# Gate sums moved from DMA to DVE, the last norm cut into 512-column pieces, and one product instead of two per sample in a hybrid decoder step

## The chip, the cores and the metric

The kernel runs on one core of one Trainium2 chip. The metric is device time in microseconds of one execution, the median of several runs. A core has five engines that run side by side and wait for one another only through semaphores: TensorE (PE in the profile; its weight loads are listed apart as PEld), VectorE (DVE), ScalarE (ACT), GpSimd (POOL) and SyncE (SP). Each takes its instructions in the order in which they were written. Transfers are issued from the queues of SP, POOL and ACT and are carried by 16 DMA engines. PE writes its results into PSUM; the others work mostly on SBUF.

## The reference

One layer of a decoder with three recurrent mixers, for a prompt of 512 tokens and for 8 samples of one token, all in fp32:

```python
p = x @ w_in                      # 2048 -> 19464 columns, split among the mixers and 3 gates
A: S_t = diag(f_t) S_{t-1} + (1 - f_t) i_t^T,   o_t = S_t^T q_t        # 8 heads, 128 x 128
B: S_t = gamma_h S_{t-1} + k_t v_t^T,           o_t = S_t^T q_t        # 4 heads, 256 x 256
C: mLSTM matrix memory with gates and a running-max stabiliser         # 4 heads, 256 x 256
y_n = head_norm(o_n) * gain * silu(z_n)
merged = sum_n sigmoid(g_n) * (y_n @ w_branch[n])
out = merged @ w_out
x_new = LayerNorm(alpha * x + out) * ln_g + ln_b
```

Outputs are the new rows of prompt and samples, and the new states of all heads, for the prompt and for each of the 8 samples.

## The kernel before

**Dense work.** The 512 prompt columns and the 8 sample columns are handled together (N = 520, halves of 260). Each fp32 operand is split into a high part `hi` and a rest `lo` in a faster format, and a product is made of three: hi*hi, hi*lo, lo*hi. ACT writes `hi`, DVE writes `lo`. The list `items` holds the dense work; an item has one weight block of 128x1024 and 24 products (a classical item 48).

The columns of `w_in` are worked in 76 units of 256 columns, in the order A, B, C, gates; the last 24 are the gates'. The first three units are plain ("classical"), all others use a Strassen scheme with seven items instead of eight: `strassen_unit` loads the two weight blocks `r1` (b11, b12) and `r2` (b21, b22), 1 MB each, into a ring of three buffers `R`, and four sums of blocks are formed. Three are formed on DVE in place. The first, `TT = b11 + b12`, is formed by DVE in the first Strassen unit and in those with interleaved columns (`deint`: q and k of B and C); in all others by two transfers: SP loads block 0 into `TT` again from DRAM, and POOL issues a transfer of block 1 that accumulates onto it. The last item of a unit takes `TT`; it is the item called `before` when the next unit is written out, and the hooks on it (0 at its start, 2 at its middle) belong to the next unit.

Then come the three branch products and the output product, as classical items of 5.74 us, and the last unit `final_unit`, which finishes the first half of the rows before the second.

**Side work.** The heads' scans and the samples' recurrences are Python generators in three queues: `prepq`, `scanq` (prompt heads), `sampq` (samples). They put small operations between the dense products. A `yield` ends a step. `side_step` is called after every third product or so of dense work and lets each queue take one step, if the planner allows it.

**The planner.** `Clock` is a model of the engines' time that runs while the program is written. Each instruction adds its price to its engine (DVE 0.11 + 0.00107 us an element, ACT 0.15 + 0.00089, a fast product 0.00046 a column, an fp32 product 0.00085) and waits for its operands as the model has them. A queue takes its next step when the model's PE has come to the queue's due time, which is the end of the last step's work plus 0.2, and only while DVE and ACT are at most 2.0 and 2.5 us beyond `clk.next`, the expected end of the present item (2.87 us after its start). The model only sets the order of the instructions; on the chip the semaphores set the time. `need` drains queues without regard to due times. `keys` cuts the large slot tensor `SL` into pieces of 520 for the model's dependences.

**Samples of B and C** (`bc_samp`, one generator per head). For a pair of samples: ACT scales v by the two halves of k into `tm` and `vb`, DVE updates the two halves (256 columns each) of the state in its slot, POOL issues the store of the state, and PE multiplies each half with `qm[e][:, b, :]`, an 8-column mask that holds q's half in column b, adding up all samples in one PSUM tile (`os`). State and v loads for the next pair are issued ahead on SP and POOL if slots are free. The 12 slots that side work shares are taken by `sl()` and given back by `fr()`. A samples (`a_samp`) have one half only. Weight loads, state loads and reloads of parked columns share SP's queue.

**The last norm** (`norm_rows`). Rows come in two halves of two 128-row blocks. After mean and variance (DVE) and the power on POOL, each block is worked in three pieces (the last in four): ACT scales, DVE multiplies by ln_g, POOL or DVE adds ln_b, SP stores. The first half runs as a side queue entry while PE works on the second half of the final unit; the second half runs in `finish`, interleaved with the samples' norm.

All operations go through one helper, so that nearly every row of the profile has line 165 (142 and 143 for transfers); rows are told apart by the tiles' names: `PD` dense PSUM, `s` and `os` PSUM of side work, `XZ` and `X` the split activations, `R`, `TT`, `hi`, `lo` the weights, `SL` the slots, `qmt` the masks, `pk_*` parked columns, `lng`, `lnb` the norm's gain and bias.

Of the kernel before, what the change touches and what calls it, by code (L numbers as in the profile page):

```python
# [39 lines left out]
class Clock:  # L40
# [4 lines left out]
    def __init__(self):  # L45
        self.t = dict(pe=0.0, dve=0.0, act=0.0, pool=0.0, sp=0.0)
        self.pipe = 0.0
        self.w, self.r = {}, {}
        self.alias = {}
        self.latest = 0.0  # L50
        self.side = False
        self.next = 0.0
# [5 lines left out]
    def keys(self, ap):  # L58
        nm = ap.name
        nm = self.alias.get(nm, nm)  # L60
        if nm.startswith(("in_", "out_", "c_")):
            return []
        cut = CHUNK.get(nm.split("_")[0])
        if cut is None:
            return [nm]
        ext = sum(abs(st) * (n - 1) for st, n in list(ap.ap)[1:])
        return [(nm, i) for i in range(ap.offset % SPAN[nm.split("_")[0]] // cut,
                                       (ap.offset % SPAN[nm.split("_")[0]] + ext) // cut + 1)]
# [50 lines left out]
class Counted:  # L119
# [3 lines left out]
    def __getattr__(self, op):  # L123
# [22 lines left out]
        def g(*a, **kw):  # L146
# [5 lines left out]
            if me == "pe":  # L152
                if op == "transpose":
                    t = 0.109 if out.shape[-1] > 64 else 0.06
                else:
                    n = a[2].shape[-1]
                    t = max(0.06, 0.00046 * n) if a[2].dtype == F32R else max(0.06, 0.00085 * n)
            elif me == "dve":
# [15 lines left out]
def tile_hybrid_step(  # L174
# [152 lines left out]
    e8 = const.tile([128, 8, 8], F32, name="e8")  # L327
    qmt = const.tile([128, 2, 8, 8], F32, name="qmt")
    ones = const.tile([128, 1], F32, name="ones")
# [92 lines left out]
    def ralloc():  # L422
        r = RT[rcount[0] % 3]
        rcount[0] += 1
        return r

    class Item:

        def __init__(self, src, mm, post=None, keep=None, nosplit=False):
            self.src, self.mm, self.post, self.hooks = src, mm, post, {}  # L430
            self.n = len(items)
            self.keep, self.nosplit = keep, nosplit
            self.late = False
            self.part = None
            items.append(self)
# [63 lines left out]

    def strassen_unit(col, deint, fin):  # L500

        src = w_in[0][:, col:col + 256]
        u = {"o": [None, None]}
# [79 lines left out]
        added = []  # L583
        if prev and not deint:
            def blk(t):
# [68 lines left out]
    def classical_rows(src, rws, xf, fin, pre=None):  # L654

        kt = 8 * rws
        for g in range(rws):
# [69 lines left out]
    def dense():  # L727
# [5 lines left out]
        for i, it in enumerate(items):  # L733
            it.run("first")
            clk.next = clk.pe + 2.87
            if i + 1 < len(items) and not items[i + 1].late:
# [70 lines left out]

    def qmask(q, e):

        t = qmt[:, e]  # L810
        V.tensor_tensor(out=t, in0=e8, in1=q.unsqueeze(2).to_broadcast([128, NS, 8]), op=MUL)
        return t

# [207 lines left out]
    def a_samp(h):  # L1021
        q, K, f, z = sm("Aq", h), sm("AK", h), sm("Af", h), sm("Az", h)
        hb = {}
        qm = qmask(q, 0)

# [218 lines left out]
    def bc_samp(h, br):  # L1244
# [34 lines left out]
        if br == 2:  # L1279
# [4 lines left out]
            for e in range(2):  # L1284
                V.tensor_tensor(out=kn[:, :, e], in0=nt[:, :, e], in1=q[e], op=MUL)
        qm = [qmask(q[e], e) for e in range(2)]
        po = po1()
        for b0 in range(0, NS, 2):
# [6 lines left out]
            for bs in ([b0, b0 + 1],) if b0 + 1 in lds else ([b0], [b0 + 1]):  # L1295
# [16 lines left out]
                for b in bs:  # L1312
# [6 lines left out]
                    G.dma_start(out=state_out[0, b, h].rearrange("(p t) v -> p t v", t=2), in_=v3(st[:, 0:512], 2))  # L1319
                fr(tm)  # L1320
                yield 1
                for b in bs:
                    st = lds.pop(b)
                    for e in range(2):
                        T.matmul(po[0:NS, 0:256], qm[e][:, b, :], st[:, e * 256:(e + 1) * 256],
                                 start=(b == 0 and e == 0), stop=(b == 7 and e == 1))
                    fr(st)
                yield 1
            fr(vb)
# [247 lines left out]

    def w_unit(col, deint, fin):
        strassen_unit(col, deint, fin)

    def plain(nm, k0):
# [35 lines left out]
    for i, (col, deint, fin) in enumerate(wl):  # L1617
        if i < NCL:
            n1 = rcount[0]
            ralloc(), ralloc()  # L1620
            classical_w(col, fin, (n1, n1 + 1))
        else:
            strassen_unit(col, deint, fin)
    first_strassen = 4 * NCL
# [101 lines left out]
    def out_setup():  # L1726
        need("Cg", *HEADS[2])
        assert len(free["h"]) == NH and len(free["d"]) == ND, (len(free["h"]), len(free["d"]))
        out["H"] = SL[:, 0:NC * D].rearrange("p (c n) -> p c n", c=NC)
        out["ot"] = [TT.rearrange("p m n -> p (m n)")[:, 0:N], smp.rearrange("p a b -> p (a b)")[:, 0:N]]  # L1730
# [36 lines left out]
    def norm_rows(c0):  # L1767
# [8 lines left out]
        yield 1  # L1776
        for c in range(2):
            hh = H[:, c0 + c, :]
            for q0, q1, e in (((0, 672, G), (672, 1344, G), (1344, 2048, V)) if c0 + c < 3 else
                              ((0, 640, G), (640, 1152, G), (1152, 1600, V), (1600, 2048, V))):  # L1780
                qq = slice(q0, q1)
                act(out=hh[:, qq], in_=hh[:, qq], func=AF.Identity, scale=r[:, c:c + 1], bias=nm[:, c:c + 1])
                V.tensor_tensor(out=hh[:, qq], in0=hh[:, qq], in1=g[:, qq], op=MUL)
                e.tensor_tensor(out=hh[:, qq], in0=hh[:, qq], in1=b[:, qq], op=ADD)
                SY.dma_start(out=y_p[0, (c0 + c) * 128:(c0 + c + 1) * 128, qq], in_=hh[:, qq])
                yield 2

# [319 lines left out]
```

## Time and profile before

| | |
|---|---|
| runs (us) | 2373.87, 2376.09, 2375.83; median 2375.83 |
| profiled execution | 2384.39 us, span 2382.5 us, mean granted TensorE clock 0.992 |
| PE busy | 2318.9 us, 97% of the span |
| DVE, ACT, POOL busy | 1603.2, 1031.3, 490.8 us |
| transfers | 449.26 MB, 189 GB/s over the span |
| last dense product ends | at about 2352.6 us |

In the profile's rows of operations, `out<-in` names the written and the read tiles, then come partitions x elements and the count; "idle before" is the time the engine stood just before such rows, with what ended the wait. The chain of waits follows the work that ended last back from the end. Times in timelines are microseconds from the start of the span.

### The profile page before, as it was taken

The page shows a single profiled execution, that of the slowest core. Times are in us where ns is not written, and L with a number is a line of the kernel's source. Part 1 is how long each engine was busy: PE and PEld are TensorE (multiplying, and loading weights), DVE is VectorE, ACT ScalarE, POOL GpSimd, SP SyncE. Part 2 cuts the span into 40 slices and gives each one's busy share as a digit, 9 for nine tenths or more (in the row PEclk, how much of TensorE's full clock was granted, in tenths as well). Part 3 has the DMA queues.
Part 4 walks back from the last instruction along what each step waited for, and adds up shares of the span by engine and source line. Part 5 has one row for each costly group of instructions (what it writes and reads, how often), then busy time and mean ns, then how long its engine had stood idle before and what let it go on. Part 6 is the DMA issues. An engine that isn't in the chain of part 4 may idle for free.

```text
span 2382.5 us, 45461 instructions
## 1 busy us (share of the span) xinstructions
PE 2318.9 (97%) x18677; PEld 2240.8 (94%) x18677; DVE 1603.2 (67%) x2571; ACT 1031.3 (43%) x1611; POOL 490.8 (21%) x653
## 2 busy tenths in 40 slices
PE   7999999999999999999999999999999999999995
PEld 7999999999999999999999899898999999999994
DVE  5777777787778868677777666767676534553336
ACT  4344445445545444454445545554554422222222
POOL 2022221323222132222122222212221100002002
PEclk9999999999999999999999999999999999999997
DMA  6367765647566576767767988889796767755221
GB/s 178 116 158 186 196 161 170 184 151 219 149 204 167 182 213 189 223 216 205 234 184 207 187 246 203 221 200 241 169 252 173 225 201 256 253 192 199 89 72 72
DMA packets 404690, 449.26 MB, mean 189 GB/s; under 512 B 16993, under 2 KB 356865, under 8 KB 402945
## 3 DMA queue, kind: packets, MB, share of 16 engines
q1 hardware_dynamic: 313664, 312.77, 42.3%
q0 software_dynamic: 90384, 133.38, 24.2%
q8 instruction: 147, 2.41, 0.4%
q14 instruction: 63, 0.51, 0.1%
q10 hardware_dynamic: 432, 0.20, 0.0%
HBM read 362.98 MB, written 83.28 MB: 187 GB/s over the span
## 4 chain that ended last, share of the span: by engine, by line
PE 61%; DMA 3%; DVE 1%; ACT 1%; issue 0%; POOL 0%; SPq 0%; DVEq 0%; POOLq 0%; ACTq 0%
PE PD L165 54%; PE s L165 4%; PE os L165 3%; DMA R<-in_w_in_dram 1%; DVE SL L165 1%; DMA out_dram<-SL 0%; DMA R<-in_w_branch_dram 0%; DMA TT<-in_w_in_dram 0%; ACT hi L165 0%; DVE lo L165 0%; ACT SL L165 0%; ACT TT L165 0%; DVE sdd L165 0%; DVE R L165 0%; DVE fmv L165 0%
## 5 line engine op out<-in xcount | busy, mean ns | idle before, releaser
L165 PE MATMUL PD<-XZ,hi 128*128 128x260 f32 x9920 | 1430.0, 285 | 13.3 <-ACT hi L165 10.0
L165 PEld LDWEIGHTS PD<-XZ,hi 128*128 128x128 f32 x9920 | 1282.7, 189 | 30.8 <-ACT hi L165 12.0
L165 DVE TENSOR_TENSOR lo<-R,hi 128x1024 fp32r<-128x1024 f32 (+1 forms) x540 | 646.1, 1198 | 381.2 <-ACT hi L165 161.6
L165 PE MATMUL PD<-XZ,lo 128*128 128x260 f32 x4944 | 799.4, 284 | 0.2 <-DVE lo L165 0.2
L165 ACT ACTIVATE hi<-R 128x1024 fp32r<-128x1024 f32 (+1 forms) x541 | 558.1, 1051 | 499.4 <-PE PD L165 254.8
L165 PEld LDWEIGHTS PD<-XZ,lo 128*128 128x128 f32 x4944 | 679.9, 189 | 5.5 <-issue 4.3
L165 ACT ACTIVATE SL<-PD 128x260 f32<-128x260 f32 x304 | 115.2, 381 | 424.3 <-PE PD L165 363.9
L165 POOL COPY smp<-SL 128x8 f32<-128x8 f32 x104 | 93.1, 895 | 535.3 <-ACT SL L165 344.2
L165 DVE TENSOR_TENSOR R<-R,R 128x1024 f32<-128x1024 f32 x146 | 178.0, 1219 | 6.4 <-DMA R<-in_w_in_dram 6.2
L165 DVE TENSOR_TENSOR SL<-SL 128x256 f32<-128x256 f32 (+9 forms) x315 | 146.4, 501 | 32.9 <-PE s L165 26.5
L165 PE MATMUL PD<-X,hi 128*128 128x260 f32 x1168 | 165.1, 287 | 0.3 <-ACT hi L165 0.3
L165 DVE TENSOR_TENSOR SL<-PD,SL 128x260 f32<-128x260 f32 x219 | 93.0, 425 | 99.4 <-PE PD L165 89.8
L165 PEld LDWEIGHTS PD<-X,hi 128*128 128x128 f32 x1168 | 148.4, 188 | 5.0 <-issue 4.1
L165 PE MATMUL s<-SL 128*128 128x64 f32 (+5 forms) x912 | 147.3, 298 | 0.0
L143 POOL DMA_DIRECT2D TT<-in_w_in_dram x56 | 90.2, 1610 | 272.7 <-DMA TT<-in_w_in_dram 245.5
L165 PEld LDWEIGHTS s<-SL 128*128 128x128 f32 (+1 forms) x912 | 125.0, 187 | 6.2
L165 ACT ACTIVATE SL<-SL 128x520 f32<-128x520 f32 (+5 forms) x156 | 85.2, 565 | 66.4 <-DVE SL L165 64.9
L142 POOL DMA_DIRECT2D out_dram<-SL x100 | 61.0, 614 | 217.9 <-DVE SL L165 196.3
L165 POOL TENSOR_TENSOR rstd<-rva,half 128x4 f32<-128x4 f32 (+3 forms) x35 | 45.2, 1292 | 247.5 <-DVE rva L165 247.4
L165 DVE TENSOR_TENSOR lo<-TT,hi 128x1024 fp32r<-128x1024 f32 x73 | 88.8, 1217 | 3.1 <-ACT hi L165 3.0
L165 DVE TENSOR_TENSOR R<-R 128x1024 f32<-128x1024 f32 x73 | 88.9, 1217 | 0.0
L165 PE MATMUL PD<-X,lo 128*128 128x260 f32 x584 | 84.7, 285 | 0.0
(213 smaller groups left out, 1416.7 us busy)
## 6 DMA issues: line engine op xcount, KB each, us to landing
R<-in_w_in_dram SPq DMA_DIRECT2D x150, 1024.0 KB, 6.3
TT<-in_w_in_dram SPq DMA_DIRECT2D x56, 512.0 KB, 6.4
TT<-in_w_in_dram POOLq DMA_DIRECT2D x56, 512.0 KB, 6.5
R<-in_w_branch_dram SPq DMA_DIRECT2D x24, 1024.0 KB, 6.5
out_dram<-SL POOLq DMA_DIRECT2D x88, 256.0 KB, 5.5
R<-in_w_out_dram SPq DMA_DIRECT2D x16, 1024.0 KB, 5.4
pk_g<-SL POOLq DMA_DIRECT2D x48, 260.0 KB, 4.7
SL<-pk_g SPq DMA_DIRECT2D x48, 260.0 KB, 5.9
```

The lines of the kernel that those rows point to most:

```text
L142: return f(out=out, in_=in_)
L143: return f(out=out, in_=in_, accum_op=accum_op)
L165: return f(*a, **kw)
```

## The change

Four things. The 24 gate units form `TT = b11 + b12` with one DVE operation at the start of the item before, instead of by the two transfers. In `bc_samp`, after the state update, two steps are added: ACT writes q's first half times the state's first half into `tm`, DVE adds q's second half times the state's second half, and PE sums `tm` over the partitions with `e8[:, b, :]`, a mask of ones; the masks with q are no longer made. `norm_rows` works every row block in four pieces of 512 columns, ACT one piece ahead, both the multiply and the addition on DVE, and takes the model's end of the work out of its due time. The planner doubles its price of an fp32 product, expects a classical item to end 5.74 us after its start instead of 2.87, and cuts `SL` at 512 in the last stage.

```diff
+        self.cut = dict(CHUNK)
-        cut = CHUNK.get(nm.split("_")[0])
+        cut = self.cut.get(nm.split("_")[0])
...
-                    t = max(0.06, 0.00046 * n) if a[2].dtype == F32R else max(0.06, 0.00085 * n)
+                    t = max(0.06, 0.00046 * n) if a[2].dtype == F32R else 2 * max(0.06, 0.00085 * n)
...
-    def strassen_unit(col, deint, fin):
+    def strassen_unit(col, deint, fin, by_dma=True):
+        span[0] = 2.87
...
-        if prev and not deint:
+        if prev and not deint and by_dma:
             def blk(t):
                 return src[:, t * 128:(t + 1) * 128].rearrange("(k e p) n -> e p k n", p=128, e=2)[0]
             items[-2].hook(0, lambda: SY.dma_start(out=TT, in_=blk(0)))
             added.append(lambda: G.dma_start(out=TT, in_=blk(1), accum_op=ADD))
         else:
             before.hook(0, lambda: add(TT, b11, b12))
...
     def classical_rows(src, rws, xf, fin, pre=None):
+        span[0] = 5.74
...
-            clk.next = clk.pe + 2.87
+            clk.next = clk.pe + it.span
...
-        qm = [qmask(q[e], e) for e in range(2)]
...
-                fr(tm)
                 yield 1
                 for b in bs:
-                    st = lds.pop(b)
-                    for e in range(2):
-                        T.matmul(po[0:NS, 0:256], qm[e][:, b, :], st[:, e * 256:(e + 1) * 256],
-                                 start=(b == 0 and e == 0), stop=(b == 7 and e == 1))
+                    i = (b % 2) * 256
+                    act(out=tm[:, i:i + 256], in_=lds[b][:, 0:256], func=AF.Copy, scale=q[0][:, b:b + 1])
+                yield 1
+                for b in bs:
+                    i, st = (b % 2) * 256, lds.pop(b)
+                    V.scalar_tensor_tensor(out=tm[:, i:i + 256], in0=st[:, 256:512], scalar=q[1][:, b:b + 1],
+                                           in1=tm[:, i:i + 256], op0=MUL, op1=ADD)
                     fr(st)
+                yield 1
+                for b in bs:
+                    i = (b % 2) * 256
+                    T.matmul(po[0:NS, 0:256], e8[:, b, :], tm[:, i:i + 256], start=(b == 0), stop=(b == 7))
+                fr(tm)
                 yield 1
...
-            strassen_unit(col, deint, fin)
+            strassen_unit(col, deint, fin, i < len(wl) - 24)
...
+        clk.cut["SL"] = 512
...
-        for c in range(2):
-            hh = H[:, c0 + c, :]
-            for q0, q1, e in (((0, 672, G), (672, 1344, G), (1344, 2048, V)) if c0 + c < 3 else
-                              ((0, 640, G), (640, 1152, G), (1152, 1600, V), (1600, 2048, V))):
-                qq = slice(q0, q1)
-                act(out=hh[:, qq], in_=hh[:, qq], func=AF.Identity, scale=r[:, c:c + 1], bias=nm[:, c:c + 1])
-                V.tensor_tensor(out=hh[:, qq], in0=hh[:, qq], in1=g[:, qq], op=MUL)
-                e.tensor_tensor(out=hh[:, qq], in0=hh[:, qq], in1=b[:, qq], op=ADD)
-                SY.dma_start(out=y_p[0, (c0 + c) * 128:(c0 + c + 1) * 128, qq], in_=hh[:, qq])
-                yield 2
+        pieces = [(c, slice(q0, q0 + 512)) for c in range(2) for q0 in range(0, D, 512)]
+        def scaled(c, qq):
+            hh = H[:, c0 + c, qq]
+            act(out=hh, in_=hh, func=AF.Identity, scale=r[:, c:c + 1], bias=nm[:, c:c + 1])
+        scaled(*pieces[0])
+        for i, (c, qq) in enumerate(pieces):
+            if i + 1 < len(pieces):
+                scaled(*pieces[i + 1])
+            hh = H[:, c0 + c, qq]
+            V.tensor_tensor(out=hh, in0=hh, in1=g[:, qq], op=MUL)
+            V.tensor_tensor(out=hh, in0=hh, in1=b[:, qq], op=ADD)
+            SY.dma_start(out=y_p[0, (c0 + c) * 128:(c0 + c + 1) * 128, qq], in_=hh)
+            clk.latest = 0.0
+            yield 1
```

More of the change, by code (lines that the diff above doesn't have):

```diff
@@ L327, in tile_hybrid_step @@
     e8 = const.tile([128, 8, 8], F32, name="e8")
-    qmt = const.tile([128, 2, 8, 8], F32, name="qmt")
+    qmt = const.tile([128, 8, 8], F32, name="qmt")
     ones = const.tile([128, 1], F32, name="ones")
@@ L425, in ralloc @@
         return r
+    span = [5.74]
     class Item:
@@ L433, in __init__ @@
             self.late = False
+            self.span = span[0]
             self.part = None
@@ L806, in put_ys, with qmask @@
         V.scalar_tensor_tensor(out=ysm[:, 8 * br + k, :], in0=psum, scalar=gains[:, br, k:k + 1], in1=z, op0=MUL, op1=MUL)
[L808 to L812, printed above, removed]
+    def qmask(q):
+        V.tensor_tensor(out=qmt, in0=e8, in1=q.unsqueeze(2).to_broadcast([128, NS, 8]), op=MUL)
+        return qmt
     def samp_silu(i0, n):
@@ L1023, in a_samp @@
         hb = {}
-        qm = qmask(q, 0)
+        qm = qmask(q)
         def get(b0):
@@ L1575, in c_head @@
         yield from room(0)
-    def w_unit(col, deint, fin):
-        strassen_unit(col, deint, fin)
     def plain(nm, k0):
@@ L1622, in tile_hybrid_step @@
         else:
-            strassen_unit(col, deint, fin)
+            strassen_unit(col, deint, fin, i < len(wl) - 24)
     first_strassen = 4 * NCL
```

## The prediction

> **What bounds the kernel now.** I read the busy table first, then the same busy times by stage, then the chain that ended last.
>
> ```profile
> PE 2318.9 (97%) x18677; PEld 2240.8 (94%) x18677; DVE 1603.2 (67%) x2571; ACT 1031.3 (43%) x1611; POOL 490.8 (21%) x653
> ```
>
> ```profile
> 450.00:810.00 360.00, 359.60 (x2972) 350.05 (x2972) 283.96 (x494) 176.12 (x309) 102.97 (x133) 1.00 0.62 178
> 810.00:1290.00 480.00, 478.95 (x3736) 452.16 (x3735) 355.17 (x522) 227.27 (x339) 119.34 (x161) 1.00 0.72 210
> 1290.00:1806.00 516.00, 504.96 (x3899) 472.86 (x3898) 358.76 (x613) 266.08 (x416) 116.47 (x153) 0.99 0.87 212
> ...
> 2353.00:2383.00 30.00, 1.72 (x7) 1.34 (x7) 24.15 (x35) 8.96 (x12) 12.94 (x8) 0.54 0.31 120
> ```
>
> Columns of a stage: its ends and length, then busy time of PE, PEld, DVE, ACT, POOL, then granted clock, DMA share, GB/s. The stages are those of the A samples, of B, of C beside the gate units, and the tail. PE never rests in the first two (0.4 and 1.1 us idle), has 11.0 us of idle beside the gates, and is done by 2353, after which DVE works through the norm for 30 us. So a product taken from PE is worth its whole length up to 2353, and an operation given to DVE or ACT costs nothing there while PE does not wait for it. In the tail it is the reverse.
>
> **The joined products.** The chain of waits shows what the products of q and the states take in PE's order:
>
> ```profile
> 1394.75 1.82 PE os L165 x8
> 1396.57 3.08 PE PD L165 x24
> ```
>
> Start, length, what. In the listing eight records are the four products of two samples (two records to an fp32 product: the group of 256 below is 128 products), and the next work starts right behind them: 1.82/4 = 0.455 us a product. B and C have 4 heads x 8 samples x 2 halves each, 128 products; half go. 64 x 0.455 = **29.1 us** less on PE. By the busy time of their group, 61.9/128 = 0.484, it would be 31.0, the upper end.
>
> What comes in: per sample one ACT scaling and one DVE multiply-add of 128x256. Their nearest rows, in the groups kept apart by shape (count, busy us, mean ns, idle before; other rows left out, here and below):
>
> ```profile
> L165 PE MATMUL os<-SL,qmt 128*8 128x256 f32 x256 | 61.9, 380 | 0.0
> L165 PE MATMUL os<-SL,qmt 128*8 128x128 f32 x128 | 16.6, 273 | 0.0
> L165 ACT ACTIVATE SL<-SL,ks 128x256 f32<-128x256 f32 x128 | 62.2, 503 | 2.5 <-DMA SL<-vs 0.4
> L165 DVE SCALAR_TENSOR_TENSOR SL<-SL,scwb 128x256 f32<-128x256 f32 x64 | 27.6, 479 | 9.2 <-DMA SL<-in_state_mlstm_c_dram 6.0 <-ACT SL L165 3.0
> L165 DVE TENSOR_TENSOR qmt<-e,smp 128x64 f32<-128x64 f32 x24 | 4.6, 218 | 0.0
> ```
>
> ACT gets 64 x 0.503 = 32.2 us, DVE 64 x 0.479 = 30.7 less 16 masks x 0.218 = 3.5. Both lie under PE's 97%. Queued behind them on DVE are the next `lo` splits, which PE needs. The new wait is PE's for ACT then DVE. PE takes its work in order, so a late sum would hold the dense products behind it. Today's products, which also follow an ACT scaling and a DVE update, have 0.0 us of idle in both rows, so the written order spaces such steps well enough. The lower end is 0; the upper takes the longest such wait that a PE product shows for ACT (next fence) once per pair, 32 x 0.73 = 23.4. I take 2, near the 0.0 rows, because the kernel's own clock prices an ACT scaling of 256 at 0.15 + 0.00089 x 256 = 0.378 where its row says 0.503.
>
> ```profile
> 1411.59 0.25 PE L165 MATMUL os<-ones,kn 128*8 128x1 f32 x4 [0.73 <-ACT SL L165]
> ```
>
> **The gates' first sums.** Each of 24 gate units drops two 512 KB loads, one on SP and one accumulating on POOL, and adds one DVE sum, which 17 units (those with interleaved columns, and the first) already make:
>
> ```profile
> L165 DVE TENSOR_TENSOR TT<-R 128x1024 f32<-128x1024 f32 x17 | 20.7, 1218 | 6.2 <-DMA R<-in_w_in_dram 6.2
> L143 POOL DMA_DIRECT2D TT<-in_w_in_dram x56 | 90.2, 1610 | 272.7 <-DMA TT<-in_w_in_dram 245.5 <-issue 16.5 <-DMA SL<-in_state_mlstm_c_dram 10.6
> TT<-in_w_in_dram SPq DMA_DIRECT2D x56, 512.0 KB, 6.4
> ```
>
> DVE: 24 x 1.218 = 29.2 us, hidden under PE. In the gate stage DVE goes from 358.8 us of 516 to about 358.8 + 29.2 + half of 27.2 = 402 of some 496, 81%; the A stage holds 284 of 360, 79%, with PE never waiting. If the cover were gone it would cost up to those 29.2. POOL loses 24 x 1.61 us of issue and 24 waits for TT, behind which its stores of states stand; SP loses 24 issues, of which each stands in front of weight and state loads. The stage loses 24 x 1.05 = 25 MB of its 212 GB/s x 516 us = 109 MB.
>
> What that is worth is what late weights cost PE there:
>
> ```profile
> 1327.98 1.34 PE L165 MATMUL PD<-XZ,hi 128*128 128x260 f32 x9 [1.44 <-ACT hi L165]
> 1381.10 2.80 PE L165 MATMUL PD<-XZ,hi 128*128 128x260 f32 x16 [1.75 <-ACT hi L165]
> 1508.84 2.18 PE L165 MATMUL PD<-XZ,hi 128*128 128x260 f32 x16 [1.21 <-ACT hi L165]
> 1637.58 3.19 PE L165 MATMUL PD<-XZ,hi 128*128 128x260 f32 x16 [3.72 <-ACT hi L165]
> ```
>
> ```profile
> 1381.10 13.65 PE PD L165 x99
> 1508.84 12.14 PE PD L165 x99
> 1618.12 11.45 DMA out_dram<-SL
> ```
>
> ```profile
> 1381.00:1385.00 4.00, 3.90 (x23) 3.91 (x24) 3.83 (x4) 2.05 (x3) 0.00 (x0) 0.67 0.76 230
> 1637.00:1641.00 4.00, 3.42 (x18) 3.42 (x19) 3.44 (x4) 2.54 (x3) 0.00 (x0) 0.67 0.93 274
> ```
>
> The first fence is PE's timeline, the second the chain, the third busy times by stage. Idle 8.1 us. After two of the four the granted clock was 0.67 for a while, and there 99 products took 13.65 instead of 12.14: 2 x 1.5 = 3.0. Together 11.1 us. In the last one, the chain runs over a state's store that took 11.45 us, then the weights: SP stood at a state load whose slot that store had to leave, with the weights behind it. So it is partly traffic, partly the order on SP. Ends: all of it gained (11.1), or, with side work bunched differently, as much lost again (-11.1). I take half, **5.5**, since one cause of the two goes.
>
> **The doubled price of fp32 products and the span of 2.87 or 5.74** move no work, only the order. The old price of a 256-column product was 0.00085 x 256 = 0.218, the chain says 0.455, the new one is 0.435: side steps come due earlier by PE's clock. Outside the gates the idle of the side-work stages is 1.5 us, so there is nothing to gain; what it can lose lies in the 23.4 above. Zero.
>
> **The tail.** The last norm, from DVE, ACT and POOL in order of time:
>
> ```profile
> 2344.07 0.95 ACT L165 ACTIVATE SL<-SL,nm,rstd 128x672 f32<-128x672 f32 x1 [3.64 <-DVE nm L165]
> 2353.61 0.42 DVE L165 SCALAR_TENSOR_TENSOR SL<-SL,s 128x256 f32<-128x256 f32 x1 [0.32 <-PE s L165]
> 2354.06 0.49 DVE L165 BATCH_NORM_STATS2 AT<-SL 128x6 f32<-128x128 f32 x2
> 2354.47 0.88 DVE L165 TENSOR_TENSOR SL<-SL,lng 128x704 f32<-128x704 f32 x1
> 2356.18 3.82 DVE L165 TENSOR_TENSOR SL<-SL,lng 128x672 f32<-128x672 f32 x3
> 2357.12 4.35 POOL L165 TENSOR_TENSOR SL<-SL,lnb 128x672 f32<-128x672 f32 x2 [6.10 <-DVE SL L165]
> 2360.04 2.17 DVE L165 TENSOR_TENSOR SL<-SL,lnb 128x704 f32<-128x704 f32 x1
> 2362.14 1.02 DVE L165 BATCH_NORM_AGGREGATE fmv<-AT 128x2 f32<-128x96 f32 x2
> 2365.43 0.86 DVE L165 TENSOR_TENSOR SL<-SL,lng 128x672 f32<-128x672 f32 x1 [0.26 <-ACT SL L165]
> 2366.20 0.15 DVE L165 COPY smu<-s 128x2 f32<-128x2 f32 x1
> 2372.92 0.29 DVE L165 TENSOR_TENSOR trit<-trit,smp 128x128 f32<-128x128 f32 x1
> 2378.59 0.62 DVE L165 TENSOR_TENSOR SL<-SL,lnb 128x448 f32<-128x448 f32 x1
> ```
>
> ```profile
> L165 DVE TENSOR_TENSOR SL<-SL 128x512 f32<-128x512 f32 x88 | 58.2, 684 | 1.4 <-ACT SL L165 1.4
> ```
>
> The second fence is the group of 512-column operations elsewhere in the kernel. In the tail a DVE operation of 0.88 takes 2.17 beside a POOL addition, and POOL's two take 4.35. The Trainium skill, "SBUF — State Buffer", section "Who interferes with whom", says a Vector instruction with two SBUF inputs and a GpSimd instruction that reads SBUF block each other; "Advanced Engine Details and Errata", "VectorE Performance Modes", names only the two-port modes, by which the stretch would not be POOL's and the tail would stay as it is, 2343 in all. The rows side with the first: both engines are slow in the same microseconds.
>
> After the change DVE does 8 pieces x 2 x 0.684 = 10.9 us for each half, ACT (some 0.8 a piece by the 0.95 of 672) being faster. The pieces no longer wait on the planner's end of the piece before, so those of the first half come out at each turn while PE finishes, and DVE runs through: from 2344.9, 10.9 and 2 x 1.1 for the two last output tiles (0.42 and 0.49 above and a copy ahead of them, small like the 0.15 below), 2358.0. That is 4.1 before the old 2362.14. From the aggregate to the first multiply it stays 3.2. The second half is 10.9 and eight small operations on the samples (first and last shown, 0.15 to 0.34, 1.7 together): 2373.8, against 2379.2 now: **5.4** less, with the landing of the last store behind both (3.3). Lower end: only two pieces of the first half before PE ends, as now; then it is 8.2 us of pieces from 2354.5, and the gain is 0.7. Upper end: the samples' 1.7 in gaps, 7.1.
>
> **The sum.** -29.1 + 2 - 5.5 + 0 - 5.4 = -38.0 on a span of 2382.5. The profiled execution took 2384.4, 8.6 above the median of the runs (2375.83), so I forecast 2375.8 - 38.0 = **2338**. The best ends give 31.0 + 11.1 + 7.1 = 49.2 (2327), the worst 29.1 - 23.4 - 11.1 + 0.7 = -4.7 (2381).
>
> **Rivals.**
> *DVE crowded beside the gates* (81%): sums and splits come late, PE waits some 0.75 us in each of 24 units, 18 us; 2356. For it: no stage shown runs that full. Against: the A stage at 79% with 0.4 us of idle, and a planner that holds side work back while DVE is ahead of PE.
> *Late weights gone altogether*: POOL and SP no longer stop at TT, the 11.1 comes back and no new wait opens; 38.0 + 5.6 + 2 = 45.6; 2330. Against: SP's state load in front of the weights is still there.
> *The joined product saves nothing beside the gates*: those stages go at the pace of DMA (share 0.87), so C's half of the products, 14.6, turns into waits; 2338 + 14.6 = 2353. Against: PE was busy 505 of 516.
> *Slower*: the new sum stands on DVE at the start of the unit's last item and waits for a weight block that is late, and the evictions, side sums and splits behind it wait with it; before, DVE met that block only half an item later. It decides from (38.0 + 4.8)/24 = 1.8 us of PE wait in each gate unit; at 2 us, 2386. For it, the waits of ACT for weights:
>
> ```profile
> ACT hi L165 <- DMA R<-in_w_in_dram: 59.1, 33, 3.8
> ```
>
> 59.1 us over 33, 1.8 each, is just that size. Against: the same sum in those 17 units stood 6.2 us in all, and the split it delays has most of an item left.
>
> **How the numbers follow.** Forecast 0.68, crowded DVE 0.12, weights all gone 0.08, C's half lost 0.07, slower 0.05. Runs of this kernel differ by some 0.1%, so I count 0.2% (4.8 us) as no change. The first four are faster, but of the crowded case a sixth (0.02) reaches no change and as much of the third falls short of 0.2% too: faster 0.91, same 0.04, slower 0.05. Range 2326 to 2357: from just under the best ends to just above the crowded case; it leaves out the slower case and the worst of the others.
>
> **What would show it.** Products on os with 256 columns: 128 records instead of 256, and each pair 0.91 us in the chain. PE busy about 29 less. No long wait of PE for `os<-`; 0.7 a pair would mean the upper end. TT: 41 DVE sums, 32 loads on SP and POOL. PE idle from the first gate to the end of C under 6 us; more than 20 means crowding. POOL with no 128x672 additions, DVE's multiplies at 0.68, and under 25 us between the last dense product and the end. The forecast is wrong if PE busy falls by 29 and the span does not.

## The result, and the profile after

The changed kernel takes **2362.9 us** (median of four runs), the kernel before 2375.4 beside it: a ratio of 0.9948, 95% interval [0.9936, 0.9959], 12.5 us faster. The forecast was 2338, with 2357 as the upper end of its range. The sign was right; two thirds of the gain did not come.

First the busy time of the engines, after:

```profile
PE 2294.3 (97%) x18549; PEld 2230.7 (94%) x18549; DVE 1649.2 (70%) x2657; ACT 1057.4 (45%) x1678; POOL 434.0 (18%) x621
```

PE has 128 records fewer and 24.6 us less to do, yet the span is only 18.6 shorter than the profiled one of before (2363.9 against 2382.5). Where the rest sits is seen by stage. The kernel before was profiled once more, as `before_again`, because the prediction had rested on one execution. The rows are busy times by stage, with the columns of the prediction: A samples, B, C beside the gate units, first gate branch and dense branch, output, tail. A stage runs from a given dense product (the 504th, 5712th, 8736th, 12264th, 15288th, 16679th) to the next, so the stages of different kernels hold the same dense work.

The kernel before, second profile:

```profile
93.80:830.80 737.00, 732.50 (x6088) 720.66 (x6087) 574.98 (x930) 351.21 (x585) 187.25 (x239) 1.00 0.63 175
830.80:1276.70 445.90, 445.90 (x3462) 419.43 (x3461) 327.47 (x485) 209.50 (x313) 110.97 (x149) 1.00 0.71 206
1276.70:1796.90 520.20, 516.96 (x4031) 485.53 (x4030) 370.00 (x625) 273.87 (x426) 121.81 (x160) 1.00 0.88 219
1796.90:2163.30 366.40, 363.65 (x3027) 363.24 (x3026) 187.44 (x257) 110.07 (x133) 32.19 (x54) 1.00 0.68 220
2163.30:2342.90 179.60, 176.14 (x1456) 173.74 (x1454) 63.19 (x128) 39.94 (x60) 10.32 (x16) 1.00 0.27 87
2342.90:2373.10 30.20, 1.96 (x10) 1.37 (x8) 24.16 (x35) 9.26 (x12) 12.95 (x8) 0.56 0.32 125
```

The changed kernel:

```profile
96.60:852.80 756.20, 744.43 (x6152) 730.56 (x6151) 586.78 (x965) 359.80 (x597) 187.95 (x246) 1.00 0.62 176
852.80:1272.30 419.50, 419.39 (x3322) 402.77 (x3321) 323.58 (x472) 214.07 (x329) 111.19 (x147) 1.00 0.74 219
1272.30:1788.30 516.00, 503.72 (x3964) 481.05 (x3963) 403.69 (x669) 285.35 (x457) 84.49 (x134) 0.99 0.57 174
1788.30:2155.50 367.20, 364.89 (x3027) 364.39 (x3026) 190.08 (x260) 109.80 (x133) 27.26 (x51) 0.99 0.61 208
2155.50:2340.20 184.70, 178.03 (x1455) 173.46 (x1454) 68.87 (x137) 43.77 (x66) 7.03 (x14) 1.00 0.27 90
2340.20:2363.90 23.70, 2.14 (x10) 1.42 (x8) 18.01 (x40) 6.14 (x9) 1.55 (x2) 0.56 0.36 136
```

Length less PE's busy time is PE's idle time. In the A stage it goes from 4.5 to 11.8 us, beside the gates from 3.2 to 12.3, in the output from 3.5 to 6.7. (The A stage is also longer because 64 side records moved into it from B.) In the first four stages together PE's busy time falls from 2059.0 to 2032.4, but the idle time rises from 10.5 to 26.5.

What PE waits for (total, times, longest), in the second profile of before and in the changed kernel:

```profile
PE PD L165 <- ACT hi L165: 0.9, 3, 0.3
```

```profile
PE PD L166 <- ACT hi L166: 15.5, 7, 7.7
...
PE s L166 <- ACT smp L166: 3.5, 9, 0.5
```

The `hi` of the first row of each is ACT's split of a weight block: dense products wait because the block came late. Two of those places in the chain of waits:

```profile
540.17 10.37 DMA R<-in_w_in_dram
...
550.56 1.06 ACT hi L166
...
551.67 3.51 PE PD L166 x27
```

```profile
1320.56 20.21 DMA R<-in_w_in_dram
...
1341.99 8.07 PE PD L166 x49
```

The page's list of transfers gives 5.9 us as the median landing of such a block; these took 10.37 and 20.21. What was issued just before the first of them, by the timeline (POOL's and SP's rows, then the waits):

```profile
538.52 0.76 POOL L143 DMA_DIRECT2D SL<-in_state_hgrn_dram  x1
539.27 0.54 POOL L143 DMA_DIRECT2D SL<-vs  x1
539.80 0.76 POOL L143 DMA_DIRECT2D SL<-in_state_hgrn_dram  x1
540.17 2.70 SPq L143 DMA_DIRECT2D R<-in_w_in_dram  x2
540.55 0.54 POOL L143 DMA_DIRECT2D SL<-vs  x1
...
551.67 2.18 PE L166 MATMUL PD<-XZ,hi 128*128 128x260 f32 x16 [2.16 <-ACT hi L166]
```

POOL's loads of an A sample's state and values go out in the same two microseconds as SP's two weight loads. Over the whole A stage, 9 of the 61 weight loads of the changed kernel have two or more such loads issued in the 3 us before them, and land after 10.3 us in the mean, the others after 6.1; in the second profile of before 1 of 61 meets that way. The Trainium skill, "DMA: Bandwidth & Descriptors", "Queues, rings and completion order", says that each DMA engine takes turns between the queues that have work for it; a weight load that shares its time with POOL's queue and lands in 10.3 instead of 6.1 agrees with that.

The second block, issued at 1320.56, stands among the transfers at the end of a C head's scan: SP issued four reloads of the head's parked columns (`pk_mo`, `pk_mz`) in the 3 us before it and three loads of sample states behind it, POOL three stores at 1319.2. Most of the long waits beside the gates lie there: in all 17 profiles of this document together, 20 of the 23 waits of PE of 2.5 us or more in that stage end 12 to 35 us after SP issued a head's `pk_mo`, stretches that make up about a sixth of the stage. Not every late block costs time: the second profile of before has a weight load of 15.3 us beside the gates (issued at 1314.6), and PE waits 0.3 us for `hi` in that whole stage.

The parts themselves look as forecast:

```profile
L166 PE MATMUL os<-SL,e x128: 379/379/383, 850.7 to 1762.6; 128*8 128x256 f32 x128
```

```profile
1381.85 0.96 PE os L166 x4
1403.63 0.96 PE os L166 x4
```

```profile
L166 DVE TENSOR_TENSOR TT<-R 128x1024 f32<-128x1024 f32 x41 | 49.9, 1218 | 9.8 <-DMA R<-in_w_in_dram 9.6
L166 PE MATMUL os<-SL,e 128*8 128x256 f32 x128 | 34.1, 380 | 0.0
L166 DVE TENSOR_TENSOR SL<-SL,lng 128x512 f32<-128x512 f32 x16 | 11.0, 684 | 1.0 <-ACT SL L166 0.9
```

First one tile's records (shortest, median and longest ns, first to last), then the chain, then the groups by shape. A pair of samples takes 0.96 on PE instead of 1.82, with no idle time ahead of the products; 41 first sums on DVE; the norm's pieces take 0.684.

### The profile page after: what moved, and what is told of

Read it like the earlier page. It is cut to its first block, busy times and chain, and to the rows that moved or that the text cites. A ratio compares the mean times of both kernels' runs of the same rounds, so it can differ in the third digit from the quotient of the medians.

```text
span 2363.9 us, 45226 instructions
## 1 busy us (share of the span) xinstructions
PE 2294.3 (97%) x18549; PEld 2230.7 (94%) x18549; DVE 1649.2 (70%) x2657; ACT 1057.4 (45%) x1678; POOL 434.0 (18%) x621
## 3 DMA queue, kind: packets, MB, share of 16 engines
q0 software_dynamic: 65424, 120.79, 18.6%
## 4 chain that ended last, share of the span: by engine, by line
PE 90%; DMA 4%; DVE 3%; ACT 1%; issue 1%; SPq 0%; POOL 0%; ACTq 0%; DVEq 0%; POOLq 0%
PE PD L166 79%; PE s L166 8%; DMA R<-in_w_in_dram 4%; PE os L166 2%; DVE SL L166 1%; DVE lo L166 1%; ACT hi L166 1%; DVE R L166 0%; DMA R<-in_w_branch_dram 0%; DMA SL<-in_x_prompt_dram 0%; DVE XZ L166 0%; ACT SL L166 0%; ACT XZ L166 0%; SPq L143 0%; ACT smp L166 0%
## 5 line engine op out<-in xcount | busy, mean ns | idle before, releaser
L166 PEld LDWEIGHTS PD<-XZ,hi 128*128 128x128 f32 x9920 | 1286.2, 189 | 38.9 <-ACT hi L166 17.6
L166 DVE TENSOR_TENSOR SL<-SL 128x256 f32<-128x256 f32 (+8 forms) x315 | 146.5, 501 | 36.2 <-PE s L166 26.6
L166 ACT ACTIVATE SL<-SL 128x512 f32<-128x512 f32 (+5 forms) x156 | 85.5, 565 | 74.7 <-DVE SL L166 69.8
L144 POOL DMA_DIRECT2D TT<-in_w_in_dram x32 | 51.3, 1602 | 154.9 <-DMA TT<-in_w_in_dram 133.0
```

The source lines that it names most:

```text
L144: return f(out=out, in_=in_, accum_op=accum_op)
L166: return f(*a, **kw)
```

## The experiments

Every run is compared with runs of the kernel before on the same chip. Not all kernels ran on one chip; where two changed kernels are compared below, the figure is the difference of their medians, and the kernel before had medians of 2375.4 to 2377.4 us beside them. For each kernel's profile I made one account from the trace: the length of the first four stages above, PE's idle time in them (the sum of the waits ahead of its records), the time lost to the granted clock (its intervals at 0.5, half of each), and the rest, which is the work. Where a wait and a slow interval overlap, the rest comes out a little low.

| kernel | time, us | ratio to before | four stages | PE idle | lost to clock | work |
|---|---|---|---|---|---|---|
| before, as first profiled | 2375.8 | | 2080.7 | 19.2 | 3.4 | 2058.0 |
| before_again | 2375.1 | 0.9991 [0.9982, 1.0001] | 2069.5 | 10.5 | 1.7 | 2057.3 |
| p_price | 2400.4 | 1.0103 [1.0088, 1.0118] | 2101.9 | 32.4 | 13.7 | 2055.9 |
| p_late | 2408.8 | 1.0132 [1.0113, 1.0150] | 2102.8 | 34.7 | 11.9 | 2056.2 |
| p_gates | 2381.0 | 1.0020 [1.0010, 1.0030] | 2073.8 | 12.6 | 3.4 | 2057.8 |
| p_norm | 2372.5 | 0.9982 [0.9973, 0.9991] | 2069.5 | 11.3 | 0.0 | 2058.2 |
| p_joined | 2367.6 | 0.9965 [0.9952, 0.9979] | 2062.5 | 26.7 | 6.8 | 2028.9 |
| the changed kernel | 2362.9 | 0.9948 [0.9936, 0.9959] | 2058.8 | 26.5 | 6.8 | 2025.5 |
| m_price | 2361.6 | 0.9937 [0.9922, 0.9952] | 2055.2 | 21.4 | 6.8 | 2026.9 |
| m_span | 2359.5 | 0.9932 [0.9917, 0.9948] | 2058.8 | 25.9 | 6.8 | 2026.1 |
| m_both | 2357.9 | 0.9925 [0.9906, 0.9945] | 2062.8 | 25.5 | 6.8 | 2030.5 |
| few_steps | 2364.0 | 0.9947 [0.9933, 0.9962] | 2064.1 | 26.4 | 10.2 | 2027.5 |
| st_pool | 2377.6 | 1.0003 [0.9994, 1.0013] | 2078.7 | 35.4 | 13.7 | 2029.6 |
| m_nogate | 2362.3 | 0.9942 [0.9925, 0.9958] | 2062.7 | 26.1 | 8.5 | 2028.1 |
| late_nogate | 2362.3 | 0.9930 [0.9906, 0.9953] | 2065.6 | 28.2 | 8.5 | 2028.9 |
| spread_a | 2352.2 | 0.9891 [0.9872, 0.9909] | 2048.9 | 17.6 | 1.7 | 2029.7 |
| **late_price** | **2343.7** | 0.9862 [0.9847, 0.9877] | 2042.0 | 10.7 | 3.4 | 2027.9 |

The last column falls into two groups: 2056 to 2058 with the old products (mean 2057.2), 2026 to 2031 with the joined ones (mean 2028.1). The joined product is worth some 29 us of work in every order. All else that separates these kernels before the output is idle time and the clock loss that comes with it.

**Was the forecast's base sound?** `before_again` is the kernel before, unchanged.

> The kernel before, once more, for a second trace of it. If the four waits for late weights beside the gates (8.1 us idle, clock down after two of them) belong to the written order, they stand again near 1328, 1381, 1509 and 1638 us. If they were an accident of the one execution that was profiled (it took 2384.4 where the runs took 2375), PE idle from the first gate to the end of C is under 5 us and the span is near 2373. Time in both cases 2375.

2375.1. The four waits beside the gates that the prediction counted at 11.1 us are not there: PE waits for `hi` 0.9 us in all, and the third stage has 3.2 us idle instead of 11.0. They belong to the one profiled execution, not to the written order. Between the two profiles the four stages differ by 11.2 us, of which 8.7 are idle time and 1.7 clock: that is why the first took 8.6 us more than the median.

**The parts alone.** `p_price` only doubles the price, `p_joined` only joins the products, `p_gates` only moves the gates' sums to DVE, `p_norm` only cuts the norm's pieces.

```diff
-  ... else max(0.06, 0.00085 * n)
+  ... else 2 * max(0.06, 0.00085 * n)
```

> The kernel before with the planner's price of fp32 products doubled, and nothing else. Theory: the new price moves the samples' loads of A into the same microseconds as the weight loads; the four waits for weights that the changed kernel shows near 474, 552, 630 and 707 us stand here too, and the time is 7 to 12 us longer, 2382 to 2387. Rival (the order does no harm, those waits came from the other parts): 2375 within 3, and no such waits.

24 us **slower**, with the same work, twice what the theory said: in the profiled execution idle time and clock loss grow by 12.8 us in the A stage, but by 22.2 beside the gates. The price makes PE's planned clock run faster, so side work is written earlier among the dense products. PE waits for `hi` 12.6 us in place of 0.9, and twice, 9.7 us in all, for a parked operand of the side work:

```profile
PE PD L165 <- ACT hi L165: 12.6, 10, 3.8
...
PE s L165 <- DMA SL<-pk_mo: 9.7, 2, 6.5
```

> The kernel before with the joined products alone, under the old prices. Theory: the 64 products are worth their whole length, PE busy falls by 29 to 31 and the time to 2344 to 2348. Rival (PE waits for the new sums, or the stages beside the gates go at the pace of the transfers): half of it or less, 2360 or more, with idle ahead of the os products.

9 us faster, a third of the forecast: the rival's time, but not its reason, for no `os` product waits. All 29 us of work are gone, but idle time and clock loss eat 21: idle 26.7 instead of 10.5, clock 6.8 instead of 1.7. With two more steps in each pair's chain C's samples run past the end of the gates: 39 more PE records in the fourth stage than before (3066 against 3027), and waits there and beside the gates. One of them, in the chain, is for a 256 KB operand that took 18.35 us to land:

```profile
1768.77 18.35 DMA SL<-pk_mo
1787.12 0.04 issue
1787.17 0.48 PE s L165
```

> The kernel before with the gates' first sums on DVE alone. The second trace of the kernel before has only 3.2 us of PE idle from the first gate to the end of C, none of it for late weights. Theory: there was next to nothing to gain, 2373 to 2378, DVE 29 us busier. Rival (the transfers taken away are worth what I forecast): 2368 to 2371. Rival (DVE holds up the last item of each unit): over 2385, with PE waits in front of dense products every 24 us.

4.7 us slower. So the sums on DVE bring nothing by themselves: in this order the DMA sums were hidden. (Of the 4.6 us between the two profiled spans, 2.0 lie in the tail, which this edit doesn't touch.)

> The kernel before with the last norm in pieces of 512 alone. Theory: as forecast, the time from the last dense product to the end falls from 30.2 to 24 us, all else is the same: 2370. Rival (POOL's share was worth having): 30 us as before, 2375.

About 4 us faster in time; its tail is 25.25 us in place of 30.2, where 24 was expected.

**The planner's two numbers undone.** `m_price` is the changed kernel with the old price, `m_span` with 2.87 for every product, `m_both` with both.

> The changed kernel with the old price of fp32 products. Theory: the waits for weights in the A stage go, the time falls by 7 to 12, to 2351 to 2356. Rival (price harmless): 2363 within 3.

> The changed kernel with 2.87 us as the expected length of every item, as before. Theory: in the output product the side steps come one item later again and PE does not stand ahead of each transpose; that stage takes 179.6 us instead of 184.7, the time is 2358. Rival (the output stage is longer by the new norm or by chance): 184.7 and 2363.

> The changed kernel with the old fp32 price and 2.87 us again for every product (so the three arithmetic edits alone). Theory (the price moves the order and brings late weights into the A stage; without it the joined chain runs past the gates): A and B stages together about 1165 us, the four one-to-two-microsecond waits on ACT hi before 710 us gone, sample products of C left over for the branch as with the price alone undone, output stage 179.5 instead of 184.7: near 2356, some 6 below the changed kernel. Rival (the parts simply add: -9 for the joined product, +5 for the gate sums, -4 for the norm): 2368.

2361.6, 2359.5 and 2357.9: the rival came for the price, the theory for the span and for both together. The span is simple: 5.74 lengthens the output stage from 179.5 to 184.7, where PE now waits for evictions into `smp` too (the 3.5 us above; 1.0 in `m_both`), and undoing it gives 3.4 us of time (5.2 in the output stage, less 1.9 in the tail). The price is not. Without it the A stage is back at 738 and its waits are gone, but C's samples spill again: in `m_both` 22 PE records on `os` stand behind the gates, 14 of them those of seven joined products (busy times of this stage, of the `os` tile alone), and the branch waits for ACT.

```profile
1772.10:2156.00 383.90, 4.87 (x22) 1.35 (x22) 1.06 (x4) 0.38 (x1) 0.99 0.64 214
```

```profile
PE PD L166 <- ACT hi L166: 14.6, 12, 4.4
...
PE PD L166 <- ACT XZ L166: 4.7, 1, 4.7
```

One order has its waits early, the other late, for nearly the same sum: 25.9 and 25.5 us idle.

**Two ways to end the spill.** `st_pool` moves the loads of B's and C's sample states from SP to POOL, `few_steps` joins ACT's scaling and DVE's add of a pair in one step; both start from `m_both`.

```diff
-            SY.dma_start(out=v3(st[:, 0:512], 2), in_=state_in[0, b, h]...
+            G.dma_start(out=v3(st[:, 0:512], 2), in_=state_in[0, b, h]...
```

> The changed kernel with the old price and 2.87 us, and with the B and C samples' state loads on POOL's queue instead of SP's. With old price and 2.87 alone I expect 2356 (the run with the old price took 2361.6, the output stage gives 5 back); it has 6.9 us of PE idle for late weights beside the gates. Theory: those weights are late because SP stands at a state load; on POOL nothing stands in front of the weights, the idle falls under 2 us and the time to 2345 to 2351. Rival (the weights are late because the transfers are full): the idle stays, 2354 to 2358.

```diff
                     act(out=tm[:, i:i + 256], in_=lds[b][:, 0:256], func=AF.Copy, scale=q[0][:, b:b + 1])
-                yield 1
                 for b in bs:
```

> The three arithmetic edits with old price and 2.87, but ScalarE's scaling and VectorE's add of one pair of samples issued in the same step (one step fewer for each pair). Theory (the longer chain of steps makes C's samples run past the gates): the last sample product ends some 30 us or more earlier than in the run with both undone, the wait of the branch on ACT XZ shrinks, and the time falls by 2 to 5 us below it. Rival (the spill is set by the price of the work, not by the count of steps): same time, within 2 us; and if the add stands in VectorE's queue behind ScalarE's scaling, PE's waits on DVE grow and it is slower.

`st_pool` missed both its theory and its rival: it lost 20 us against `m_both`, and PE waits for `hi` 24.3 us. `few_steps` did end C's samples some 100 us earlier (their last output is written at 1791.5 instead of 1890.9), as the theory said, and was still 6 us slower: idle time in the branch fell from 8.5 to 1.8 us, but three waits of 3.3 to 5.6 stand beside the gates. The first of them is a joined product's for the add on DVE, which the rival had named; the other two are for weights. Other side work spilled in the samples' place: 3124 PE records in the fourth stage instead of 3072. So ending the samples earlier doesn't win the lost time by itself.

**The price where the new products are.** `late_price` is the changed kernel with 2.87 everywhere, and the doubled price only from the first sample of B and C on.

```diff
+        self.fp = 1.0
...
-  ... else 2 * max(0.06, 0.00085 * n)
+  ... else c.fp * max(0.06, 0.00085 * n)
...
     def bc_samp(h, br):
+        clk.fp = 2.0
```

> The changed kernel with 2.87 us again for every product, and the doubled fp32 price in force only from the first sample of B and C on, so that the A stage is written as in the kernel before and B and C as in the changed one. Theory: the late weights of the A stage go (idle there 4 to 5 us instead of 11.8) and the samples still end inside the gates (no waits in the branch beyond 3 us): 2350 to 2356. Rival (the idle time of the A stage is not the price's): as the changed kernel with 2.87, 2359.5. Other rival (the order shifts as a whole, so C spills as with the old price): near the run with both undone.

**2343.7**, ratio 0.9862 [0.9847, 0.9877]: 31.9 us faster than the kernel before and, by the medians of the two comparisons, 19.2 faster than the changed one, with the same products on PE. Its stages and its waits for `hi`:

```profile
91.90:829.40 737.50, 732.56 (x6089) 720.63 (x6088) 574.95 (x929) 351.74 (x585) 187.90 (x239) 1.00 0.63 175
829.40:1261.00 431.60, 431.02 (x3396) 413.65 (x3395) 336.87 (x504) 220.78 (x343) 116.06 (x150) 1.00 0.73 213
1261.00:1766.60 505.60, 502.96 (x3970) 479.74 (x3969) 407.47 (x678) 288.31 (x460) 90.15 (x139) 1.00 0.59 183
```

```profile
PE PD L167 <- ACT hi L167: 1.2, 4, 0.4
```

The A stage is that of before (4.9 idle), C beside the gates has 2.6 us of idle in place of 12.3, and nothing spills. That is 6 us and more below the theory, which named only the A stage: against `m_span` 6.7 us of idle went there, as it said, but 9.5 from C beside the gates, where the price is the same in both. Nobody forecast that part. DVE is as busy there as in the changed kernel (407 of 506 us), so DVE was not what cost the time.

> The kernel before, with the fp32 price doubled from the first sample of B and C on and nothing else. Theory (a price moves the order, and any order that wasn't fitted to it gets late weights, though most of the 25 us of the doubling throughout came from the A stage): the A stage as before at 737 us, C beside the gates 5 to 8 us longer, 2378 to 2383. Rival (only the A stage minds the price): 2375 to 2377. Other rival (the doubled price is right for these products and orders B and C better): below 2373.

The same price on the kernel before costs 31 us, four times the expectation's upper difference. A stage as before (738.2), and 24.2 us idle beside the gates. So the doubled price is not good or bad for B and C by itself: with the joined products it belongs to the best order that I ran, with the old ones to the worst. The chain at its longest wait shows how one is made:

```profile
1594.37 12.94 DMA out_dram<-SL
...
1607.79 6.42 DMA R<-in_w_in_dram
...
1615.43 6.65 PE PD L166 x41
```

The store of a state takes 12.94 us; SP stands at a load that needs its buffer, and the weights behind it on SP are issued only at 1607.8, though they then land in 6.4.

**The gates' sums in other orders, and one step more.** `m_nogate` is `m_span`, `late_nogate` is `late_price`, each with the sums on the DMA as before. `spread_a` is `m_span` with one step between POOL's two loads of an A sample.

> The changed kernel with 2.87 us again, and the gates' first weight sums on the DMA as before. The gate sums alone made the old kernel 4.7 us slower. If that holds beside the joined product too: about 2355, 4 to 5 below the same kernel with the sums on DVE (2359.5). Rival (in the changed order the three weight blocks on SP and POOL are late beside more side work, as forecast, so the sums on DVE do save here): 2362 to 2366.

> The best order so far (price doubled only from the first sample of B and C on, 2.87 us for every product), with the gates' first weight sums on the DMA as before. Theory (in an order without late weights the DMA sums are hidden and the sums on VectorE only stand before the products; alone they made the old kernel 4.7 us slower): 2339 to 2342, 2 to 5 below the 2343.7 with the sums on VectorE. Rival (with the joined products PE reaches the gates' next weights sooner and the queue on SP and POOL is the limit, as forecast): 2346 to 2350.

2.8 us more than with the sums on DVE in the one order (the rival's number, but within what these runs can tell), 18.6 more in the other (some 17 by the two ratios), beyond theory and rival. There the loss is mostly one operand, late by another such path:

```profile
1709.59 19.22 DMA SL<-pk_mo
...
1728.86 0.47 PE s L167
```

With +4.7 alone for the opposite step, the edit has no price of its own that these runs show; it shifts the order, and the order decides.

```diff
             G.dma_start(out=v3(st[:, 0:512], 4), in_=state_hgrn[0, b0:b0 + 4, h]...
+            yield 1
             G.dma_start(out=v3(vb[:, 0:512], 4), in_=vs_d[0][h * 8 + b0:h * 8 + b0 + 4, :]...
```

> The changed kernel with 2.87 us for every product, doubled price throughout, and one step of side work between POOL's loads of an A sample's state and of its values. Theory (the four waits of the A stage near 472, 549, 627 and 705 us come from those two loads sharing the DMA engines with two weight loads just issued): the four waits of 1.3 to 1.6 us shrink or vanish, the weights there land in about 6 us after issue instead of 10, and the A stage is 4 to 6 us shorter: 2354 to 2356. Rival (the weights are issued late by SP's queue and POOL's loads are beside the point): the four waits stay and the time is 2359 to 2361.

2352.2, 7.3 below `m_span`, near the theory's number, but only a part of it for its reason. At two of the four places the loads no longer meet the weights, and there the waits are gone. Near 472 three of POOL's four loads now go out behind the weights:

```profile
458.81 0.78 POOL L143 DMA_DIRECT2D SL<-in_state_hgrn_dram  x1
461.46 1.53 SPq L143 DMA_DIRECT2D R<-in_w_in_dram  x2
465.44 0.57 POOL L143 DMA_DIRECT2D SL<-vs  x1
465.98 0.78 POOL L143 DMA_DIRECT2D SL<-in_state_hgrn_dram  x1
466.73 0.56 POOL L143 DMA_DIRECT2D SL<-vs  x1
```

The first of these weight loads lands after 5.2 us, where it took 10.0 in `m_span`. Near 549 POOL issues none beside them, and the first lands after 5.1 instead of 9.8. At the other two places the loads did not move apart (near 620 POOL issues them at 608.53, 609.29, 609.82 and 610.57, SP the weights at 610.19), and the weights are as late as ever:

```profile
610.19 9.68 DMA R<-in_w_in_dram
...
621.08 3.51 PE PD L166 x27
```

The waits remain there (1.07 and 1.72). So at all four places late weights and PE's waits come and go with POOL's loads beside them. No run took these loads away and left all else as it was, so this is strong evidence and not yet proof. Of 8.3 us of idle that went, though, only 2.7 went from the A stage and 7.9 from C beside the gates, which the edit doesn't touch (other stages gained some). Most of this gain is again what a shift by one step does to the rest of the order.

## Why the prediction was right and wrong

**The step that failed** is "The doubled price of fp32 products and the span of 2.87 or 5.74 move no work, only the order ... Zero". The order was the expensive part. The account of the changed kernel against the second profile of before, in spans (2373.1 to 2363.9, -9.2): work -31.8, idle time and clock loss in the four stages +21.1, output +5.1, tail -6.5, the start +2.8 (16 side records moved there, so that some 2 us of the work only changed place). The argument for zero was that the idle time outside the gates was small, "so there is nothing to gain"; that says nothing of what a new order can lose, and the bound of 23.4 for that loss was tied to the `os` products, which show 0.0 of idle. The 21 us came by another way: weight blocks and parked operands that land 10 to 20 us after their issue, behind or beside other loads, or are issued late behind a load that waits for a store. It is not this edit alone that brings them: with the old price and the old span, `p_joined` and `m_both` lose as much (26.7 and 25.5 us idle in the four stages, against 10.5). So the failure is wider than that paragraph: nowhere in the sum, the 2 us of the joined products' own waits included, is there a term for the waits that dense products meet in a newly written order. `late_price`, which changes the planner's numbers and nothing else, gets 15.8 us of time back against `m_span`, and 3.4 more come with the span.

- *The joined product, -29.1*: right in size (0.96 for a pair where 0.91 was taken; 27 to 32 us of work in all eleven orders, 29 in the mean), and its group went from 61.9 to 34.1.
- *New waits of PE, +2*: right for what it named: in the changed kernel no `os<-SL,e` product waits (in the other ten orders three of them do, 3.3 us the longest).
- *The gates' sums, -5.5*: wrong at its base. The 11.1 us it halved belong to one execution, and were already missing from the median to which the sum was added. The ordinary runs had nothing there to gain, and the edit alone cost 4.7, while in the two orders with joined products that were tried the sums on the DMA took 2.8 and 18.6 more.
- *The tail, -5.4*: -6.5 in the changed kernel, -5.0 with the norm alone, by the steps described; 23.7 us after the last dense product, where under 25 was said. The last 1.5 to 2 of the 6.5 come with the span of 5.74: without it the tail takes 25.2 to 26.0 in all orders with the new norm.
- *The output*: the prediction treated 5.74 as order only; it cost 5.1.

Without the two failed terms the sum is 2375.8 - 29.1 + 2 - 5.4 = 2343.3, and the order that keeps idle time as before gives 2343.7. By size the terms held; what failed was to take an order as free. That the two agree to 0.4 us is partly luck: the four runs of `late_price` spread from 2340.4 to 2344.4, and it keeps the gates' sums on DVE, whose effect changes with the order.

Of the rivals, *DVE crowded* fell (78% beside the gates, 404 of 516 us; the waits are for weights), and so did *slower* (the 41 first sums wait 9.6 us for weights on DVE, 0.2 each). *The joined product saves nothing beside the gates* was near in price (14.6 forecast; idle time and clock loss grew by 12.5 there) but not in reason: the DMA share of that stage fell from 0.88 to 0.57. Of the signs that were named, "PE idle from the first gate to the end of C under 6" failed at 12.3, and "PE busy falls by 29 and the span does not" is close to what came: 24.6 by the page, in which products at half clock count as busy.

**What stays open**: why a given order meets late loads and another does not. The runs show single cases (POOL's loads beside the weights, SP behind a store, a parked operand of 18 to 20 us) and that most of those beside the gates lie at the end of a C head's scan, not a rule that would have picked `late_price` beforehand; `p_late` and `late_nogate` missed their theories by 20 us or more.

## What to carry to other kernels

In a kernel whose order is written by a planner's prices, treat a price as an edit of the whole schedule: time it alone, and beside the edits that it comes with: the same price, in force from the same place on, came with the fastest kernel here and with the slowest. Take a product's saving from PE's work, and book beside it the idle time that a new order may bring, bounded by runs of other orders and not by the waits of the present one. Before a wait is counted as a gain, look whether a second profile of the same kernel has it.

## What the runs showed of the hardware

The granted clock falls to half after quite short waits. In the 17 profiles, from 100 to 2250 us, each of the 29 waits of PE of 2.65 us or more has an interval at 0.5 that starts between 6.0 us before the wait's end and 3.5 after it, of 3.41, 6.83 or 10.24 us; of 76 waits of 1.25 to 2.6 us 17 have one, of 41 between 0.9 and 1.25 none. In the 3.41 us before each of the 46 intervals PE had been idle for 1.6 us or more in all. So, by my estimate, a late load that PE waits 3 us for costs nearer to 5: half of an interval of 3.41 comes on top. The Trainium skill, "TensorE: Matmul & The Clock Gate", "What's actually happening", names one idle window of about 3.4 us for the fall; the unit of 3.41 agrees with the intervals here, but idle time of half that length was enough at times.

A 256 KB load took 18.35 us in one kernel and 19.22 in another, where the median of its eight is 8.4 and 5.3, and a 1 MB load 20.21, where it is 5.9; a change of one step in the written order, or of one price, moves which loads these are, and with it the time by 0.3% (a step) to 1.3% (a price).
